# Turning the first group's queries inside the loop over the second group's products

## The chip, the cores and the metric

The kernel runs on one core of a Trainium2 chip. The metric is the device time of one execution in microseconds (us); lower is better. Three runs of the kernel before gave a median of 1921.63 us.

## The reference

The reference is a two-layer decoder trunk over 512 tokens and 16 meta tokens, width 1024. Layer 0 mixes tokens by gated linear attention; layer 1, which the change concerns, by sliding-window attention. Each layer is a SwiGLU block, the mixer and another SwiGLU block, each between two RMS norms, and everything is added to a residual. The mixer of layer 1, cut to what matters:

```python
def swa_mixer(hn, w_q, sinks, w_out, k, v, cos, sin):
    q = (hn @ w_q).reshape(B, L, N_KV_HEADS, GROUP, HEAD_DIM)
    q = apply_partial_rope(q, cos, sin) * HEAD_DIM ** -0.5      # first 16 of 64 columns are turned
    s = einsum(q_blk, k_band)        # own 128 keys, the 128 before, 16 meta keys
    p = sink_softmax(s, mask, sinks) # row maximum, exp, sum with a sink per head
    o = einsum(p, v_band)
    return o @ w_out
```

There are 16 query heads of 64 columns. Keys and values are made earlier and are shared.

## The kernel before

All activations lie transposed in on-chip memory: partitions are features, columns are tokens. A weight arrives by DMA in a `raw` buffer (eight of them), and ScalarE and VectorE make two rounded halves of it (L230 and L231, one pair of instructions for each half unit of 128x512); a product is then three matmuls (`mm3s`, L338).

The order of instructions on TensorE is written by hand, and a small planner (`Flow`, L64) decides what comes next. Jobs are Python generators. Each yields an estimated delay or another job to wait for, and `flow.clock` advances by an estimated cost per matmul. When a job's due time has come, its next step is recorded at that place, between two of the matmuls that the main thread is recording. So constants such as `GATHER`, `TURN` and `PROBS` (L50 to L52) are not waits on the chip: they move instructions to earlier or later places of every queue, TensorE's, VectorE's (DVE), ScalarE's (ACT), GpSimd's (POOL) and SyncE's (SP) alike. On the chip each engine works through its queue in order and waits on semaphores where data is not there yet.

The mixer of layer 1 is `swa` (L1121). Its steps:

1. `x_first` (L534) makes the queries of the first four of eight units (a unit is 128 features, that is two heads), for token group 0 (256 tokens) and then for group 1. After each group it spawns `drain`, which copies the four results from PSUM to `q` tiles on ACT (`evac`, L1145).
2. `turn` (L1148) applies the rotary turn to one half of the units and one group. It waits for the drain, then `GATHER`; four small matmuls with `sel` gather the 16 turned rows of each head in one PSUM tile, four DVE instructions turn them (L1159 to L1163), and eight DMAs on the SP queue put the rows back in the `q` tiles (L1167). It ends `TURN` later. Its first DVE instruction stands behind the last `x_l1m` operand that DVE builds (`after`, L1160).
3. `x_units` (L1289) makes the queries of the other four units, 512 tokens at a time: 32 steps of three matmuls. `turn(1, ...)` follows.
4. `attend(i)` is spawned for 16 visits. A visit is one unit and one half of the tokens; visits 0 to 3 are units 0 to 3 on the first half, 4 to 7 the same units on the second half, 8 to 15 the other units in the same way. `soft(i)` records the scores (16 matmuls into `sa` and `sb` tiles), two ACT copies (L1202), two DVE merges (L1203), the sink column and row maximum (L1215 to L1217), four exponentials on ACT (L1219) and the normalisation on DVE (L1224 to L1228). `core(i)` records, `NORM` after that, five transposes (L178, tiles `ptm` and `pt`), two ACT copies out of PSUM (L1240, L1248), one masked DVE copy (L1250), then, `PROBS` later, the products with the values (tile `o`) and the split of the result into `so` (L422 on ACT, L423 on DVE).
5. `out_proj` runs over units 0 to 3 when cores 0 to 7 have been recorded, and over units 4 to 7 at the end, where `Residual.run` puts in the row sums `st_post` and the factors `r_post`. Remaining visits are fed in between its matmuls.

Visit i's part on TensorE is called S(i) (its scores), T(i) (its transposes) and O(i) (its products with the values) below. They are recorded wherever the planner's clock says, and TensorE takes them in that order.

Of the kernel before, what the change touches and what calls it, by code (L numbers as in the profile page):

```python
# [29 lines left out]
L1 = [(16, 256), (272, 256)]  # L30
# [16 lines left out]
NORM = 5.0  # L47
LAG = 5
PERIOD = 4.5
GATHER = 3.0  # L50
TURN = 9.0
PROBS = 2.5  # L52
NEG = -1e30

V_GAIN = 0
# [72 lines left out]
def trunk_kernel(ctx: ExitStack, tc, a, out):  # L128
    nc = tc.nc
    pe, act, dve, pool, sp = nc.tensor, nc.scalar, nc.vector, nc.gpsimd, nc.sync  # L130
    flow = Flow()
# [16 lines left out]
    def ps(name):  # L148
        return pp.tile([P, 512], F32, tag="ps", name=name)
# [4 lines left out]
    def duo(name):  # L154
        t = pair_tile(name, F32)
        return t[:, 0], t[:, 1]
# [4 lines left out]
    def gain(layer, i, k):  # L161
        c = V_GAIN + layer * 48 + i * 8 + k
        return vec[:, c : c + 1]

    def mm(o, lhs, rhs, start=True, stop=True, onto=False, cost=None):
        inst = pe.matmul(o, lhs, rhs, start=start, stop=stop, skip_group_check=onto)  # L166
        n = 1
        for d in rhs.shape[1:]:
            n *= d
        flow.clock += cost or (n / 2400 if rhs.dtype == F32R else max(n / 600, 0.12))  # L170
        return inst

    def after(first, then):
        info = mybir.DependencyInfo(mybir.DependencyClass.NoSync, mybir.DependencyReason.DATA)
        tc.add_manual_dep(then.ins, first.ins.name, info, reason="order")
# [37 lines left out]
    def set_ahead(n, slots=None):  # L213
        ahead[0], limit[0] = n, slots or n
        room[0].finish(flow)
        room[0] = Job(None)
# [87 lines left out]
    def prefetch():  # L304
        while len(loaded) < cap[0] and asked[0] + costs[len(loaded)] <= freed[0] + ahead[0]:
            if isinstance(units[len(loaded)], list) and chains[0] == CHAINS:
                break
            load_unit()

    def next_w():  # L310
        used[0] += 1
        prefetch()
        flow.until(lambda: len(loaded) >= used[0])
        flow.wait(split_jobs[used[0] - 1])
        return loaded[used[0] - 1]
# [16 lines left out]
    def done_w(n=1):  # L332
        free_slots(sum(costs[released[0] : released[0] + n]))
        released[0] += n
# [3 lines left out]
    def mm3s(outs, j, x, g, start, stop, shared=False):  # L338
        t, n = g
        cols = slice(j % 4 * P, (j % 4 + 1) * P)  # L340
        xh, xl = x[:, 0, t : t + n], x[:, 1, t : t + n]
        for i, (o, w) in enumerate(outs):
            second = shared and i % 2 == 1
            mm(o, w[j // 4][:, 0, cols], xh, start and not second, False, second)
            mm(o, w[j // 4][:, 1, cols], xh, False, False, second)
        for i, (o, w) in enumerate(outs):
            second = shared and i % 2 == 1
            mm(o, w[j // 4][:, 0, cols], xl, False, stop, second)
            flow.pump()
# [181 lines left out]
        return late  # L531


    def x_first(x, nu, evac, opening=False, behind=(), first_ahead=8, held=None):  # L534
        behind = list(behind)
        ws = [] if opening else [next_w() for _ in range(nu)]
        set_ahead(8 if opening else 2 * first_ahead, held)
        jobs = []

        def drain(gi, g, some, pst):  # L540
            if x.column is None:
                yield x.rjob[gi]
            for i, p in zip(some, pst):
                evac(i, g, p)
                yield 0.6

        both = range(nu)
        order = [(0, both[: nu // 2]), (0, both[nu // 2 :])] if opening else [(0, both)]
        for gi, some in order + [(1, both)]:
            g = x.groups[gi]  # L550
            n = g[1]
            while len(ws) <= some[-1]:
                ws.append(next_w())
            shared = n <= 256
            if shared:
                banks = [ps(f"x{used[0]}_{i}_{gi}") for i in some[::2]]
                pst = [banks[i // 2][:, i % 2 * 256 : i % 2 * 256 + n] for i in range(len(some))]
            else:
                pst = [ps(f"x{used[0]}_{i}_{gi}")[:, :n] for i in some]
            for k in range(KD):  # L560
                x.need(gi, k)
                mm3s([(p, ws[i]) for i, p in zip(some, pst)], k, x.tiles[k], g, k == 0, k == KD - 1, shared)
            if x.column is None:
                flow.until(lambda: x.rjob[gi] is not None)
            jobs.append(flow.spawn(drain(gi, g, some, pst)))
            if gi == 0 and some[-1] == nu - 1:
                if held is None:
                    cap[0] = len(units)
                prefetch()
            if behind:  # L570
                flow.spawn(behind.pop(0))
        done_w(nu)
        return jobs
# [267 lines left out]
    def gla(x, finish):  # L841
        set_ahead(10)
        with tc.tile_pool(name="gp", bufs=1) as gp:
# [193 lines left out]

            kinds = [("lr", 0), ("k", 0), ("q", 0), ("v", 0)]
            drained = x_first(x, 4, lambda i, g, p: evac(*kinds[i], g, p), first_ahead=5)
            flow.spawn(resets())  # L1040
            gate = flow.spawn(gates(drained))
# [23 lines left out]
    def shared_kv(x, kp, behind):  # L1065
# [22 lines left out]
        def place(drained):  # L1088
# [26 lines left out]
            dve.tensor_tensor(dv, vt[:, 1:], vt[:, :3], op=ALU.subtract)  # L1115

        job = flow.spawn(place(x_first(x, 4, evac, behind=behind, first_ahead=6)))
        return (kz, vt, dv, vmz), job


    def swa(x, kv, finish):  # L1121
        kz, vt, dv, vmz = kv
        cap[0] = used[0] + 8
        with tc.tile_pool(name="ap", bufs=1) as ap:
# [23 lines left out]
            def turn(half, g, after_jobs):  # L1148
                for jb in after_jobs:
                    yield jb  # L1150
                yield GATHER
                o, n = g
                pk, sh = (t[:, o : o + n] for t in duo(f"turn{half}_{o}"))
                p = ps(f"turn{half}_{o}")[:, :n]
                for u in range(4):
                    mm(p[32 * u : 32 * u + 32], sel, qd[2 * half + u // 2][:, u % 2, o : o + n], cost=0.2)
                while (1, KD - 1) not in x.ready:
                    yield SCORE
                first = dve.stream_shuffle(sh, p, TURN_SHUFFLE)  # L1159
                after(x.built, first)  # L1160
                dve.tensor_tensor(pk, p, cr[:, o : o + n], op=ALU.mult)
                dve.tensor_tensor(sh, sh, sr[:, o : o + n], op=ALU.mult)
                dve.tensor_tensor(pk, pk, sh, op=ALU.add)  # L1163
                for u in range(4):
                    for e in range(2):
                        rows = qd[2 * half + u // 2][64 * e : 64 * e + 16, u % 2, o : o + n]
                        sp.dma_start(rows, pk[32 * u + 16 * e : 32 * u + 16 * e + 16])  # L1167
                yield TURN

# [61 lines left out]
            def core(i):  # L1231
# [18 lines left out]
                dve.tensor_tensor(own(ptc), own(pb), mle.unsqueeze(1).to_broadcast([P, 4 if hf else 2, P]), op=ALU.mult)  # L1250
                yield PROBS
                o = ps(f"o{u}_{hf}")
# [28 lines left out]
                paces.append(flow.spawn(pace(wait)))  # L1281
                cores.append(flow.spawn(core(i)))

            drained = x_first(x, 4, evac, held=12)
            set_ahead(16, 8)
            turns = [flow.spawn(turn(0, g, [drained[gi]])) for gi, g in enumerate(L1)]
            for i in range(8):
                attend(i, turns[i // 4], *cores[max(i - LAG, 0) : max(i - LAG + 1, 0)])
            x_units(x, 4, L1W, lambda i, g, p: evac(4 + i, g, p))  # L1289
# [16 lines left out]
    x = Operand("l0f0", lambda k: gain(0, 0, k), L0)  # L1306
# [54 lines left out]
    x = nxt  # L1361
    nxt, fin = into("l0f1", 0, 3, False, lambda k: gain(0, 4, k), L0)
    gla(x, fin)
    x = nxt
# [4 lines left out]
    with tc.tile_pool(name="kp", bufs=1) as kp:  # L1369
        x = Operand("l1f0", lambda k: gain(1, 0, k), L1)  # L1370

        def again(gi):
            for k in range(KD):
                x.build(gi, k)
                yield 1.0

        kv, placed = shared_kv(nxt, kp, [again(0), again(1)])
        x.rt, x.rjob = nxt.rt, nxt.rjob
        nxt, fin = into("l1m", 1, 1, True, lambda k: gain(1, 2, k), L1)
        roots = kp.tile([P, 2, 4], F32, name="roots")  # L1380
        nxt.column = [(roots[:, 0, 2 * g : 2 * g + 2], roots[:, 1, 2 * g : 2 * g + 2]) for g in range(2)]
        ffn(x, L1W, fin)
        x = nxt
        nxt, fin = into("l1f1", 1, 3, False, lambda k: gain(1, 4, k), L1)
        flow.wait(placed)
        swa(x, kv, fin)
# [91 lines left out]
```

## Time and profile before

| what | value |
|---|---|
| median of three runs | 1921.63 us (1921.38 to 1921.96) |
| profiled execution, its own time | 1919.54 us |
| span of its trace | 1917.7 us |
| granted TensorE clock, mean over the span | 0.994 |
| TensorE matmul busy | 1889.3 us, 99% |
| VectorE (DVE) busy | 1397.6 us, 73% |
| ScalarE (ACT) busy | 1016.4 us, 53% |
| GpSimd (POOL) busy | 178.9 us, 9% |
| DMA | 175.13 MB, mean 91 GB/s |

The profile is of one execution. Its own time is 2.1 us below the median of the runs, and the span is 1.8 us shorter than its time. "Idle before" is the time in which an engine had nothing to do ahead of an instruction, with what released it. The granted clock is the share of full speed at which TensorE was clocked. In the trace, a matmul of float32 operands appears as several records, so counts there are above those in the code; a busy TensorE is not TensorE at its peak.

The mixer of layer 1 stands between about 1388 us (its first query products) and 1550 us (the first products of the block behind it).

### The profile page before, as it was taken

The numbers are of one execution on the slowest core, as the hardware profiler recorded it, in microseconds if no ns is written. First come the engines' busy times: TensorE is split into PE (matmuls) and PEld (weight loads), VectorE is DVE, ScalarE is ACT, GpSimd is POOL, SyncE is SP. The second block draws the span as 40 slices with busy tenths as digits, with TensorE's granted clock in tenths as the row PEclk, the third lists the DMA queues.
The fourth block names the chain that finished last, engine by engine and source line by source line (L and its number), as shares of the span: only waits on it lengthen the run. The fifth ranks groups of instructions, "written<-read, shape, count | busy, mean of one in ns | idle before, by whom it ended". The sixth has DMA issues, their size and how long they took to land.

```text
span 1917.7 us, 37635 instructions
## 1 busy us (share of the span) xinstructions
PE 1889.3 (99%) x14658; PEld 1800.2 (94%) x14658; DVE 1397.6 (73%) x2803; ACT 1016.4 (53%) x2262; POOL 178.9 (9%) x379
## 2 busy tenths in 40 slices
PE   8999999999999999999999999999998999999997
PEld 8999999999999999999999898989986798989897
DVE  7885858665565788585878786868757678868584
ACT  5663636653246566363664553636647765636363
POOL 2000000321121300000031000000310040000002
PEclk9999999999999999999999999999998999999998
DMA  4332333322113123232341223333311212333331
GB/s 166 98 102 91 104 95 108 113 77 68 56 56 100 56 89 103 92 105 91 115 150 45 72 92 107 102 102 115 129 29 51 89 41 76 96 105 108 102 114 45
DMA packets 102932, 175.13 MB, mean 91 GB/s; under 512 B 11873, under 2 KB 24929, under 8 KB 102753
## 3 DMA queue, kind: packets, MB, share of 16 engines
q1 hardware_dynamic: 101920, 172.07, 28.5%
q8 instruction: 115, 1.88, 0.4%
q10 hardware_dynamic: 832, 0.65, 0.1%
q14 instruction: 65, 0.52, 0.1%
HBM read 170.05 MB, written 2.10 MB: 90 GB/s over the span
## 4 chain that ended last, share of the span: by engine, by line
PE 86%; DVE 9%; ACT 3%; issue 2%; DMA 1%; POOL 0%; SPq 0%; DVEq 0%; ACTq 0%
PE y L166 30%; PE x L166 18%; PE a L166 18%; PE c L166 8%; PE d L166 4%; DVE raw L255 2%; ACT w_s L249 1%; DVE w_s L250 1%; DVE w L250 1%; PE o L166 1%; PE e L166 1%; DVE w L231 1%; PE po L166 1%; PE ps L166 0%; DVE hidl1f L834 0%
## 5 line engine op out<-in xcount | busy, mean ns | idle before, releaser
L250 DVE TENSOR_TENSOR w_s<-raw,w_s 128x512 fp32r<-128x512 f32 x288 | 193.9, 690 | 130.0 <-ACT w_s L249 128.3
L166 PE MATMUL y<-hidl0f,w 128*128 128x256 f32 (+1 forms) x2112 | 261.9, 285 | 0.9 <-DVE hidl0f L423 0.6
L166 PEld LDWEIGHTS y<-hidl0f,w 128*128 128x128 f32 x2112 | 259.1, 188 | 1.6 <-DVE hidl0f L423 1.0
L249 ACT ACTIVATE w_s<-raw 128x512 fp32r<-128x512 f32 x288 | 175.3, 628 | 150.5 <-DVE raw L255 137.3
L231 DVE TENSOR_TENSOR w<-raw,w 128x512 fp32r<-128x512 f32 x378 | 236.3, 655 | 21.0 <-ACT w L230 19.0
L166 PE MATMUL y<-hidl1f,w 128*128 128x512 f32 (+1 forms) x1344 | 251.0, 346 | 0.3 <-DVE hidl1f L834 0.2
L166 PEld LDWEIGHTS y<-hidl1f,w 128*128 128x128 f32 x1344 | 212.3, 188 | 35.2 <-DVE hidl1f L834 1.5
L230 ACT ACTIVATE w<-raw 128x512 fp32r<-128x512 f32 x378 | 207.4, 586 | 41.1 <-PE y L166 30.4
L255 DVE TENSOR_TENSOR raw<-raw,raw 128x512 f32<-128x512 f32 x288 | 197.9, 687 | 5.6
L418 POOL TENSOR_TENSOR acc_post<-acc_post,sq_post 128x256 f32<-128x256 f32 (+1 forms) x72 | 58.9, 818 | 1469.4 <-ACT sq_post L417 1468.6
L250 DVE TENSOR_TENSOR w<-raw,w 128x512 fp32r<-128x512 f32 x216 | 148.2, 687 | 29.9 <-ACT w L249 29.2
L166 PE MATMUL x<-x_l0m,w 128*128 128x272 f32 (+1 forms) x1200 | 158.2, 288 | 0.0
L249 ACT ACTIVATE w<-raw 128x512 fp32r<-128x512 f32 x216 | 134.0, 621 | 41.3 <-PE y L166 41.0
L166 PEld LDWEIGHTS x<-x_l0m,w 128*128 128x128 f32 x1200 | 149.3, 189 | 1.1
L613 DVE TENSOR_TENSOR Y<-y,Y 128x256 f32<-128x256 f32 (+2 forms) x176 | 82.2, 473 | 71.9 <-PE y L166 71.5
L166 PE MATMUL a<-zl0f_t,w_s 128*128 128x264 f32 x864 | 117.5, 285 | 0.0
L166 PE MATMUL a<-zl1f_t,w_s 128*128 128x256 f32 x864 | 114.4, 281 | 0.9 <-ACT c L809 0.6
L166 PEld LDWEIGHTS a<-zl0f_t,w_s 128*128 128x128 f32 x864 | 110.3, 188 | 0.2
L166 PEld LDWEIGHTS a<-zl1f_t,w_s 128*128 128x128 f32 x864 | 107.2, 188 | 2.8 <-ACT c L809 2.4
L166 PE MATMUL x<-x_l0f,w 128*128 128x256 f32 (+1 forms) x768 | 100.5, 291 | 6.5 <-ACT w L230 5.9
L166 PEld LDWEIGHTS x<-x_l0f,w 128*128 128x128 f32 x768 | 97.1, 193 | 7.8 <-ACT w L230 5.9
L166 PE MATMUL x<-x_l1f,w 128*128 128x256 f32 (+1 forms) x576 | 92.6, 320 | 0.0
(484 smaller groups left out, 3250.8 us busy)
## 6 DMA issues: line engine op xcount, KB each, us to landing
raw<-in_w_in SPq DMA_DIRECT2D x352, 256.0 KB, 2.9
raw<-in_w_out SPq DMA_DIRECT2D x96, 256.0 KB, 3.3
raw<-in_gla_in SPq DMA_DIRECT2D x50, 256.0 KB, 3.1
raw<-in_w_last SPq DMA_DIRECT2D x48, 256.0 KB, 3.1
raw<-in_w_out SPq DMA_DIRECT2D x64, 128.0 KB, 2.9
raw<-in_gla_out SPq DMA_DIRECT2D x16, 256.0 KB, 2.8
raw<-in_w_q SPq DMA_DIRECT2D x16, 256.0 KB, 3.7
raw<-in_swa_out SPq DMA_DIRECT2D x16, 256.0 KB, 3.3
```

The lines of the kernel that those rows point to most:

```text
L166: inst = pe.matmul(o, lhs, rhs, start=start, stop=stop, skip_group_check=onto)
L230: act.activation(w[:, 0, :m], raw[:, :m], AF.Copy)
L231: dve.tensor_tensor(w[:, 1, :m], raw[:, :m], w[:, 0, :m].bitcast(F32), op=ALU.subtract)
L249: act.activation(w[:, 0, :512], src, AF.Copy)
L250: dve.tensor_tensor(w[:, 1, :512], src, w[:, 0, :512].bitcast(F32), op=ALU.subtract)
L255: dve.tensor_tensor(dst, dst, src, op=ALU.add)
L418: pool.tensor_tensor(sums[0][:, :n], sums[0][:, :n], t[:, :n], op=ALU.add)
L613: dve.tensor_tensor(y, p[:, :n], y, op=ALU.add)
```

## The change

`x_first` gets a callback, `then`, that it calls right after it has spawned a group's drain. `swa` uses it to spawn `turn` for that group at once. For group 0 this is ahead of the loop over group 1's products, for group 1 behind it. Before, both turns were spawned after `x_first` had returned. Three planner constants are changed too.

```diff
-GATHER = 3.0
-TURN = 9.0
-PROBS = 2.5
+GATHER = 2.0
+TURN = 8.5
+PROBS = 3.2
...
-    def x_first(x, nu, evac, opening=False, behind=(), first_ahead=8, held=None):
+    def x_first(x, nu, evac, opening=False, behind=(), first_ahead=8, held=None, then=lambda gi, job: None):
...
             jobs.append(flow.spawn(drain(gi, g, some, pst)))
+            then(gi, jobs[-1])
...
-            drained = x_first(x, 4, evac, held=12)
+            turns = []
+            x_first(x, 4, evac, held=12, then=lambda gi, job: turns.append(flow.spawn(turn(0, L1[gi], [job]))))
             set_ahead(16, 8)
-            turns = [flow.spawn(turn(0, g, [drained[gi]])) for gi, g in enumerate(L1)]
             for i in range(8):
                 attend(i, turns[i // 4], *cores[max(i - LAG, 0) : max(i - LAG + 1, 0)])
```

No instruction is added or removed. What changes is where the instructions of the turns, of the visits, and of some weight splits and loads stand in the queues of the engines. Behind L565 the lines of the changed kernel are numbered one higher, and behind L1286 again as before.

## The prediction

> **What bounds the kernel now.** I read the page's slices first (TensorE busy in nine tenths or more of nearly every slice), then three stretches of the mixer of layer 1: the query products with two scores among them, the visits with no large product beside them, and the visits among the output products.
>
> ```profile
> core 0: us, PE busy (x) PEld busy (x) DVE busy (x) ACT busy (x) POOL busy (x), PEclk, DMA share, GB/s
> 1404.20:1431.70 27.50, 27.50 (x156) 20.80 (x154) 7.86 (x23) 9.22 (x26) 2.34 (x12) 1.00 0.04 10
> 1431.70:1475.80 44.10, 37.74 (x369) 25.82 (x368) 36.05 (x96) 34.63 (x117) 0.00 (x0) 0.88 0.17 55
> 1475.80:1549.60 73.80, 73.24 (x596) 59.53 (x595) 45.31 (x117) 51.82 (x145) 8.78 (x12) 1.00 0.18 58
> ```
>
> Only in the middle stretch is TensorE idle (6.4 us) and slowly clocked (0.88), with DVE and ACT busy for 36.05 and 34.63 of 44.1 us. Its timeline shows the gaps:
>
> ```profile
> 1437.64 0.44 PE L166 MATMUL o<-pt,dv 128*64 128x128 f32 x4 [0.69 <-DVE pt L1250]
> ...
> 1443.41 0.69 PE L166 MATMUL o<-pt,vt 128*64 128x128 f32 x4 [1.37 <-ACT pt L1248]
> ...
> 1463.81 0.44 PE L166 MATMUL o<-pt,vt 128*64 128x128 f32 x4 [1.55 <-ACT pt L1248]
> ```
>
> O waits for the copies of what T put in PSUM. After such gaps the clock falls (the same columns, 2 us each):
>
> ```profile
> 1440.00:1442.00 2.00, 1.69 (x14) 1.35 (x14) 2.00 (x6) 2.00 (x6) 0.00 (x0) 1.00 0.89 257
> 1442.00:1444.00 2.00, 0.63 (x5) 0.30 (x4) 2.00 (x5) 1.94 (x6) 0.00 (x0) 0.65 0.93 318
> 1444.00:1446.00 2.00, 1.94 (x14) 0.88 (x12) 2.00 (x7) 1.02 (x5) 0.00 (x0) 0.50 0.93 327
> 1446.00:1448.00 2.00, 2.00 (x13) 1.31 (x11) 1.86 (x6) 1.51 (x8) 0.00 (x0) 0.50 0.68 215
> 1448.00:1450.00 2.00, 2.00 (x20) 1.80 (x20) 0.60 (x4) 0.95 (x3) 0.00 (x0) 0.65 0.23 51
> ```
>
> The lost shares (0.35+0.5+0.5+0.35) make 6.8 us at half clock from 1442.6; rows at 1466 and 1468 (0.62, 0.53) make 3.4 us more from 1466.5. In the 3.4 us ahead of each, 1.3 and 1.4 us are idle. At half clock an O took 3.25 us instead of 1.69, an S 1.87 instead of 1.14, a T 1.20 instead of 0.67.
>
> **The change, part by part.** The amount of work is the same; the sum is over what becomes idle or slow. The new places are those in which the built programs hold their instructions.
>
> *The first turn.* Its four matmuls move from among unit 4's products to group 1's products, some 18 matmuls of 0.12 us before their end, so to about 1402. TensorE executes them either way (0.57 us): nothing. Their data is old (copies end 1394.8). DVE is idle from 1402 to 1410, which hides the four turns (1.5 us), with one weight split now among them; two units' splits now stand behind the operand builds, finished by about 1406, and their weights are needed from 1419. Should that cover fail, TensorE waits at most for those, some 2 us. On SP five of eight `swa_out` loads pass ahead of the eight turn DMAs, three behind them; these loads are split only after 1435. The first DMA starts near 1404.8 and lands 1.8 us (median) later; S(0) is not reached before 1412.7, so 6 us of cover.
>
> *The visits.* S(0) moves from 1419.96 to about 1412.7 (first group's end 1404.8, sums 0.8, 27 matmuls of 0.241, a turn 0.57). Now S(0) to S(3), all of visit 0 and T(1) lie among query products, against S(0) and S(1) before. With T 0.67, S 1.14, O 1.69 (first half) or 1.91, the products end near 1436.3.
>
> *The order of a visit.* Before, TensorE took T(i), S(i+3), O(i): 1.14 us of scores beside the copies of T. Now, without a product near, it takes T(i), O(i), S(i+3). O(i) waits for ACT's copy (0.6) and for the masked copy on DVE, which starts only after that copy (1457.96 after 1456.73). What decides are the queues of DVE and ACT, worked out with these rows:
>
> ```profile
> 1458.56 0.15 DVE L1217 TENSOR_TENSOR nm<-nm,roots 128x4 f32<-128x4 f32 x1
> 1458.63 0.77 DVE L1203 COPY_PREDICATED s<-mgt,sb 128x256 f32<-128x256 int32 x2
> 1459.43 0.17 DVE L1215 TENSOR_TENSOR s<-vec,roots 128x4 f32<-128x4 f32 x1
> 1459.63 0.76 DVE L1216 TENSOR_REDUCE nm<-s 128x4 f32<-128x580 f32 x1
> 1460.42 0.16 DVE L1217 TENSOR_TENSOR nm<-nm,roots 128x4 f32<-128x4 f32 x1
> 1460.91 0.18 DVE L1224 RECIPROCAL den<-den 128x4 f32<-128x4 f32 x1 [0.33 <-ACT Y L1219]
> ```
>
> DVE: turn and splits first. From 1438.2 it has turn(1) 1.8+0.6, eight splits at 0.61, two merges at 0.67, two O splits at 0.33, two masked copies at 0.33, a reduction 0.67, a normalisation 0.6 and small ones 0.5: 11.7 us without a gap, to 1450.2, when masked copy 3 is done. Before, it was done at 1453.6: the start is 3.4 us ahead. Then one visit's loop, in DVE's new order from one masked copy to the next: reduction 0.79; 0.25 to the exponentials; 2.10 to the reciprocal (1458.81 to 1460.91); it, the mean row and the O split 0.75; two merges 0.67; normalisation 0.6 and sinks 0.1; masked copy 0.6: 5.8 us. DVE waits out the exponentials in each loop, since nothing stands between maximum and reciprocal; before, the previous visit's masked copy or the next one's merges often did, and the four loops to masked copy 7 took 5.1 us each (1453.6 to 1474.1). Now 1450.2 + 4 x 5.8 = 1473.4. O(7) follows the masked copy with 1.55 us, so the output products start at 1475.05, not 1475.83; but S(10), 1.14 us, was done by then and is not now. Net +0.4 us: the lead is spent in the loops. The bounds: loops of 5.1 as measured give -2.4; a wait for ACT of 0.3 us in each gives +1.6.
>
> *The end.* T(15) now stands behind all but six of the first group's matmuls (0.73 us), and the row sums `st_post` directly after these and ahead of O(15). They need the last `Y`, which DVE adds only behind masked copy 15. From T's end: ACT's queue and copy 0.9, masked copy 0.6, add 0.34, ACT's square 0.2+0.4 and latencies 0.3, so 2.7 us; TensorE arrives after 0.73: +1.9 us. Before, O(15) and 21 matmuls hid this chain; no gap is shown there. Bounds 1.2 (if the copy is early) to 3.
>
> *The clock.* Each loop of 5.8 us holds about 2.0 us of idle TensorE (1.2 before O, 0.8 between its halves), and 1441.6 to 1449.7 holds 4.7. The first certainly crosses the 1.3 to 1.4 us in 3.4 that was enough before; the loops do in about half of the phases. A slow O(3) delays the exponentials queued behind its split on ACT: +1.5 (3.25 less 1.69). A slow loop has scores 1.6 and O 2.6 on its path and grows by 1.25, four loops half of the time +2.5; the wait at `st_post` may cost 1 more. That is 5.0 at most likely phases, nothing if the clock holds. I take 3.0: the gaps are spread more evenly than the old ones, one of which (1.24 us in 3.4) did not slow the clock.
>
> Sum: +0.4 +1.9 +3.0 = +5.3 us on an own time of 1919.54 (span 1917.7 and 1.8 around it), so 1924.8; the median of runs lies 2.1 above this execution, so **1927.0**.
>
> **Rivals.** *The clock stays full*: if only one gap of a whole 3.4 us counted, no new gap (longest 2 us, before T(3)) would slow it: +0.4+1.9 = +2.3, 1923.9. Against it: the longest old gap is 1.55 us and the clock fell twice. [...]
>
> *Faster*: ACT and DVE overlap as before and TensorE sets the pace. A loop is then 0.67+0.9+1.69 to 1.91+1.14, 4.6 us; four from 1450.2 end at 1468.6, 5.5 us ahead of before; less S(10), and with `st_post` fed early, -4.4: 1917.2. For it: the lead of 3.4 us is real. Against: DVE's order. It decides if masked copies come under 5 us apart.
>
> *A lost cover in front* (the turn late on SP or DVE, TensorE waiting in group 1's products): up to 2 us more, 1929. Against: 6 us of cover.
>
> *No effect*: the early turn only makes S(0) earlier and the gaps merely shift; the change does not do what it says: 1921.6. Against: four scores instead of two under the products.
>
> **How the numbers follow.** 0.2% is 3.8 us, about what a measurement can tell from no change. Forecast 0.52, clock stays full 0.25, faster 0.15, lost cover 0.05, no effect 0.03. Forecast and lost cover lie beyond +3.8 but for 0.02 of them: slower 0.55; same 0.30 with the clock's rival and no effect; faster 0.15. The forecast's own range is 1925 to 1931 (clock terms 1 to 7); 1918.5 to 1931.5 takes in the clock's rival, the front's cost and the better part of the faster case.
>
> **What would show it.** S(0) near 1412.7; O(3) to O(7) with a gap ahead of each from ACT's or DVE's `pt`; masked copies 5.8 us apart or more; granted clock at half for three or more windows of 3.4 us after 1441; a gap of about 2 us at `st_post`. Masked copies 5 us apart, or a full clock, would make it wrong.

## The result, and the profile after

The changed kernel takes 1934.58 us (median of six runs, 1933.42 to 1936.33), the kernel before 1921.6 us on the same chip: 13.0 us more, a ratio of 1.0069 with a 95% interval of 1.0056 to 1.0081. The direction was forecast; the size was not (1927.0, range 1918.5 to 1931.5).

The profiled execution took 1936.33 us of its own time (span 1934.5), 16.8 more than that of before; its mean granted clock is 0.987 against 0.994. It is the longest of the six, and the one of before lies 2.1 us below its median, so the traces show somewhat more loss than the medians. The three stretches of the mixer, cut at the same marks as before (end of the first group's products, end of the query products, first output product, first product of the next block):

```profile
core 0: us, PE busy (x) PEld busy (x) DVE busy (x) ACT busy (x) POOL busy (x), PEclk, DMA share, GB/s
1404.96:1436.90 31.94, 31.94 (x209) 24.71 (x207) 14.30 (x40) 15.70 (x46) 2.78 (x12) 1.00 0.15 42
1436.90:1481.38 44.48, 35.56 (x291) 23.17 (x291) 29.20 (x76) 29.38 (x97) 0.00 (x0) 0.74 0.18 54
1481.38:1567.13 85.75, 82.14 (x612) 66.67 (x611) 49.48 (x126) 53.19 (x147) 10.21 (x14) 0.90 0.16 50
```

The first stretch has no gap; it ends 5.2 us later than before because more of the visits lies in it. The second should have become shorter by as much, and did not: TensorE idles for 8.9 us in it (6.4 before) at a clock of 0.74 (0.88). The third grew from 73.8 to 85.75 us, of which 1.14 is S(10), moved into it; it now has 3.6 us of idle and a clock of 0.90, where before had 0.56 and 1.00. The next block then starts 17.5 us late (1567.13 against 1549.65), of which 16.8 us are left at the end.

The gaps, from TensorE's timeline (start, duration, engine, line; in brackets the idle time and what ended it):

```profile
1449.71 0.69 PE L166 MATMUL o<-pt,vt 128*64 128x128 f32 x4 [0.69 <-ACT pt L1249]
...
1471.96 0.44 PE L166 MATMUL o<-pt,vt 128*64 128x128 f32 x4 [0.69 <-ACT pt L1249]
...
1477.21 0.44 PE L166 MATMUL o<-pt,vt 128*64 128x128 f32 x4 [0.97 <-ACT pt L1249]
1478.46 0.69 PE L166 MATMUL o<-pt,dv 128*64 128x128 f32 x4 [0.81 <-DVE pt L1251]
...
1532.43 0.44 PE L166 MATMUL o<-pt,vt 128*64 128x128 f32 x4 [1.99 <-ACT pt L1249]
1533.20 0.69 PE L166 MATMUL o<-pt,dv 128*64 128x128 f32 x4 [0.33 <-DVE pt L1251]
...
1549.66 1.00 PE L166 MATMUL st_post_l1f<-ones,acc_post 128*128 128x1 f32 x6 [1.28 <-ACT acc_post L414]
```

O(3), O(6) and O(7) wait as foretold (these are their rows; O(4) and O(5) do too), and so does `st_post`. The longest single wait, 1.99 us ahead of O(13), was in no part of the prediction. The granted clock in rows of 2 us, same columns as above:

```profile
1446.00:1448.00 2.00, 0.33 (x2) 0.20 (x3) 2.00 (x5) 2.00 (x9) 0.00 (x0) 0.94 0.80 267
1448.00:1450.00 2.00, 1.31 (x8) 0.91 (x8) 2.00 (x6) 1.32 (x4) 0.00 (x0) 0.50 0.85 260
1450.00:1452.00 2.00, 2.00 (x16) 1.01 (x12) 1.39 (x7) 0.00 (x0) 0.00 (x0) 0.50 0.74 249
...
1532.00:1534.00 2.00, 1.24 (x10) 0.67 (x12) 1.93 (x6) 2.00 (x6) 0.74 (x1) 0.78 0.90 307
1534.00:1536.00 2.00, 2.00 (x16) 1.13 (x16) 1.81 (x3) 1.14 (x3) 0.72 (x1) 0.50 0.65 237
```

Such rows give the spans at half clock: from 1447.8 (6.8 us), 1458.0 (13.7), 1478.5 (6.8), 1533.1 (6.8, behind O(13)'s wait) and 1550.2 (6.8, behind `st_post`'s). That is 41 us, against 10.2 before. The starts lie 10.2, 20.5, 54.6 and 17.1 us apart, which is 3, 6, 16 and 5 steps of 3.41 us: in this trace the clock falls on a fixed grid, so whether a gap counts may depend on where it lies on that grid.

What half clock does to a visit's loop is to be seen on DVE, from one masked copy (L1251) to the next:

```profile
1464.22 0.69 DVE L1251 TENSOR_TENSOR pt<-pt,mle 128x512 f32<-128x512 f32 x1 [0.34 <-ACT pt L1249]
1464.83 0.75 DVE L1217 TENSOR_REDUCE nm<-s 128x4 f32<-128x580 f32 x1
1465.61 0.16 DVE L1218 TENSOR_TENSOR nm<-nm,roots 128x4 f32<-128x4 f32 x1
1467.97 0.18 DVE L1225 RECIPROCAL den<-den 128x4 f32<-128x4 f32 x1 [2.20 <-ACT s L1220]
...
1470.17 0.79 DVE L1204 COPY_PREDICATED s<-mgt,sb 128x256 f32<-128x256 int32 x2 [1.32 <-PE sb L166]
...
1471.94 0.69 DVE L1251 TENSOR_TENSOR pt<-pt,mle 128x512 f32<-128x512 f32 x1 [0.34 <-ACT pt L1249]
```

DVE waits out the exponentials (2.20), as foretold, and then once more, 1.32 us, for the scores: behind O, at half clock, they come later than the exponentials end. The loop is 7.72 us long; those from masked copy 3 on were 6.9, 7.4, 7.7 and 5.8.

### The profile page after: what moved, and what is told of

Its sections match the earlier page's. It is cut to its first block, busy times and chain, and to the rows that moved or that the text cites. A ratio compares the mean times of both kernels' runs of the same rounds, so it can differ in the third digit from the quotient of the medians.

```text
span 1934.5 us, 37618 instructions
## 1 busy us (share of the span) xinstructions
PE 1900.3 (98%) x14658; PEld 1807.9 (93%) x14658; DVE 1397.4 (72%) x2803; ACT 1017.5 (53%) x2262; POOL 179.3 (9%) x379
## 4 chain that ended last, share of the span: by engine, by line
PE 85%; DVE 9%; ACT 3%; issue 1%; POOL 0%; DMA 0%; SPq 0%; DVEq 0%; ACTq 0%; POOLq 0%
PE y L166 29%; PE x L166 18%; PE a L166 18%; PE c L166 8%; PE d L166 4%; DVE raw L255 2%; PE o L166 2%; ACT w_s L249 1%; DVE w_s L250 1%; DVE w L250 1%; PE e L166 1%; DVE w L231 1%; PE po L166 1%; PE sa L166 1%; PE ps L166 0%
```

## The experiments

The theory after the result: the early turn itself costs nothing; early turn and new constants together turn TensorE's order from T, S, O to T, O, S where no large product hides it, and put waits at the end; the gaps then pull the clock down, and that costs more than the gaps. Each run below is compared with the kernel before on its own chip (1919.64 us for the first four, 1919.74 for the next four, 1919.99 for the last two).

**The early turn with the old constants.** Edit:

```diff
-GATHER = 2.0
-TURN = 8.5
-PROBS = 3.2
+GATHER = 3.0
+TURN = 9.0
+PROBS = 2.5
```

> The early turn with the three constants of before (GATHER 3.0, TURN 9.0, PROBS 2.5). In its program the stretch without products runs T(i), S(i+3), O(i) again, as before, and st_post stands three matmuls behind O(15), past the row-sum chain. Theory A (the order T, O, S and the late end, both made by the constants, cost the time; the early turn itself costs nothing): 1916 to 1923 us, at most 7 us of half clock between 1437 and 1480, no gap at O(13). Rival B (the early turn itself costs, by what it pushes in front of the visits): within 3 us of the changed kernel's 1934.6.

1917.48 us, ratio 0.9986 (0.9977 to 0.9995). This kernel beats both: the early turn alone is a small gain of 2.2 us (1 to 4 by the interval). TensorE's order is T, S, O again, and the output products start at 1474.16, 1.7 us ahead of before.

**The new constants without the early turn.** Edit: the three constants of the change in the kernel before.

> The three new constants (GATHER 2.0, TURN 8.5, PROBS 3.2) with the turn spawned where it was before. In its program the stretch without products still runs T, S, O. Theory A (order): 1919 to 1925 us, as the old kernel, since the constants alone do not turn the order round. Rival B (early turn costs): the same 1919 to 1925. Rival C (the constants cost wherever the turn stands, for example PROBS 3.2 by the later T(14) and T(15)): 1927 or more.

1919.06 us, ratio 0.9995 (0.9986 to 1.0004): nothing that can be measured. Neither half of the change costs time; only both together do.

**Filling the gaps, first trial.** Matmuls of a tile of zeros, 0.128 us each (0.06 had been expected), into columns of the `ptm` and `o` banks that hold no result yet. Edit:

```diff
+            def fill(bank, n, first=True):
+                for k in range(n):
+                    mm(bank[:, 256:384], zeros, zeros, first, False, onto=True, cost=1e-9)
...
+                if i == 3:
+                    fill(pm, 18)
...
+                if 2 <= i < 8:
+                    fill(o, 12)
...
+                    if 4 <= i < 8 and c == 0:
+                        fill(o, 10, False)
```

> The changed kernel with small matmuls of zeros into unused columns of PSUM tiles: 12 ahead of O(2) to O(7), 10 between the halves of O(4) to O(7), 18 ahead of T(3), about 0.06 us each, so 0.6 to 1.1 us into gaps of 0.7 to 1.2 us. Nothing else is moved. If the half clock is a price of its own beside the idle time: the granted clock stays at 1.00 from 1437 to 1480, the output products start near 1476 instead of 1481.4, and the time falls by 4 to 7 us, to 1928 to 1931. If the waits for DVE and ACT are all there is: no gain, or up to 2 us slower by the added matmuls.

1934.04 us, ratio 1.0073 (1.0057 to 1.0088): no gain, though the clock's mean rose to 0.994. The trace shows why this run decides nothing. The fills were longer than the gaps: from 1460 us on, at full clock, the loops are 6.41 us, without a gap, all TensorE. And they moved ACT's queue: the copy of T(3) came behind four exponentials,

```profile
1454.54 0.69 PE L166 MATMUL o<-pt,vt 128*64 128x128 f32 x4 [4.69 <-ACT pt L1255]
```

and O(3) waited 4.69 us for it. It is repeated below with short fills.

**The row sums later.** Edit: one planner delay of the residual behind the mixer is longer, so `st_post` of the first group is recorded behind O(15). The delay holds for the second group too, whose row sums also move back.

```diff
-            yield 1.8
+            yield 3.0 if self.name == "l1f1" else 1.8
```

> The changed kernel with one planner delay raised from 1.8 to 3.0 for the residual behind the mixer, which moves st_post from ahead of O(15) to three matmuls of the second token group behind it; the rest of TensorE's order is the same. If st_post's wait costs what the trace shows there (1.3 us idle and 6.8 us at half clock behind it): 3 to 4.5 us less than the changed kernel, 1930 to 1931.5. If only the idle counts: 1 to 1.5 us less. If the wait is hidden by what follows: no change within 0.7 us.

1934.78 us, ratio 1.0070 (1.0053 to 1.0087): no change. The wait at `st_post` and the half clock behind it are gone, and the next block starts at 1561.98 instead of 1567.13 us. But 23 us into that block its products wait for their operand, which a chain from the row sums builds (waits of 0.39 and 0.30 us stand shortly ahead of this one):

```profile
1589.25 4.61 PE L166 MATMUL x<-x_l1f,w 128*128 128x256 f32 x18 [1.66 <-ACT x_l1f L442]
```

and the clock falls for 3.4 us there. The wait was moved, not removed. In the trace 48 TensorE records of the next block stand ahead of the second group's row sums, 33 in the changed kernel, so this edit may itself have made the later wait; the run doesn't tell what the wait at `st_post` alone costs.

**The new order in the stretch, the old end.** Edit: `PROBS` back to 2.5, the other two constants as changed. 24 output products stand between T(13) and O(13) instead of 33, twelve between T(15) and O(15), the row sums behind O(15); up to O(7) TensorE's order is that of the changed kernel.

> The changed kernel with PROBS back at 2.5, GATHER 2.0 and TURN 8.5 kept. TensorE still takes T(i), O(i), S(i+3) in the stretch with no large product beside it (that half of the new order is kept), while from T(13) on its order is that of the early turn with the old constants: 24 output products between T(13) and O(13), 12 between T(15) and O(15), the row sums behind O(15). Theory 'both halves pay': the output products start about 5.5 us late as in the changed kernel (near 1481), but the 2.0 us before O(13), the 1.3 us before the row sums and the two half-clock spans of 6.8 us behind them are gone (about 3.3 of idle, 1.1 to 1.9 us lost to each slow span): 1927 to 1929. Rival 'the end is all': the late start of the output products is made up later, 1919 to 1922. Rival 'the stretch is all': the end's waits were hidden by work that was late anyway, 1933 to 1935.

1926.73 us, ratio 1.0032 (1.0019 to 1.0044), just below the 1927 to 1929 of 'both halves pay'. Against its kernel before that is +7.0 where the changed kernel has +13.0: 6.0 us of the loss were at the end. Its stages (same columns; the cuts are the first output product and the next block):

```profile
1436.90:1479.89 42.99, 33.76 (x297) 21.91 (x294) 29.57 (x79) 29.33 (x97) 0.00 (x0) 0.81 0.18 56
1479.89:1557.52 77.63, 76.80 (x612) 61.76 (x611) 48.58 (x124) 52.79 (x146) 9.74 (x13) 0.97 0.17 56
```

In O(13) there is one wait of 0.72 us, none at `st_post`, no half clock behind 1484; the first row is nearly as slow as in the changed kernel (1.5 us shorter).

**The old order in the stretch, `PROBS` new.** Edit: `GATHER` and `TURN` back to 3.0 and 9.0, `PROBS` 3.2 kept.

> The changed kernel with GATHER and TURN back at 3.0 and 9.0, PROBS kept at 3.2. TensorE takes T(i), S(i+3), O(i) in the stretch, as before the change; the end is between the two: 27 products between T(13) and O(13), 24 between T(15) and O(15), the row sums 6 products behind O(15). Theory 'the order T, O, S in the stretch starts the loss': the output products start as with the early turn and the old constants (near 1474 to 1475) and hardly any time is lost behind them: 1917 to 1920. Rival 'PROBS at 3.2 makes the loss by what it does to the end': 1923 to 1929. Rival 'nothing but the early turn counts': 1917.5 exactly as with the old constants.

1918.37 us, ratio 0.9990 (0.9981 to 0.9999). TensorE's order is T, S, O, there is no gap behind 1470, and the loss is gone. The output products start at 1476.46, later than expected, behind two spans of 6.8 us at half clock, and that costs nothing that can be measured. So with the early turn `GATHER` and `TURN` decide the order in the stretch; `PROBS` at 3.2 does harm only together with them, and then behind the stretch.

**Short fills.** The changed kernel with the fills of the first trial cut to the gaps' size; ACT's and DVE's queues keep their order but for a few neighbours. Edit, against the first trial:

```diff
+FILL_O = {2: 6, 3: 5, 4: 6, 5: 6, 6: 6, 7: 6, 13: 12}
+FILL_M = {4: 4, 5: 4, 6: 4, 7: 4}
...
-                if i == 3:
-                    fill(pm, 18)
...
-                if 2 <= i < 8:
-                    fill(o, 12)
+                fill(o, FILL_O.get(i, 0))
...
-                    if 4 <= i < 8 and c == 0:
-                        fill(o, 10, False)
+                    if c == 0:
+                        fill(o, FILL_M.get(i, 0), False)
```

> The changed kernel with short runs of matmuls of a tile of zeros into unused columns of the o bank (0.128 us each): five or six ahead of O(2) to O(7), four between the halves of O(4) to O(7), twelve ahead of O(13). They add 6.5 us of TensorE work, all of it in places where TensorE stood idle in the changed kernel; ACT's and DVE's queues keep their order but for a few neighbours behind visit 7 (the first trial with fills was longer than the gaps and moved the exponentials ahead of the copies of T(3)). Theory 'the half clock has a price of its own': without gaps the clock stays full, the loops come down from 6.9 to 7.7 us to about 6, the output products start near 1476 and the spans of half clock behind them are gone: 1923 to 1927. Rival 'the queues of DVE and ACT set the loops, whatever the clock': loops of about 7 us stay, 1933 to 1936.

1926.27 us, ratio 1.0032 (1.0021 to 1.0043). The fills are 63 matmuls or 8 us more of work on TensorE, and the loss against the kernel before is 6.5 us instead of 13.0. The profiled execution took 1932.67 us, 6.4 above the median, with 27 us at half clock, so its rows don't stand for the median; still, two of its loops, from masked copy 4 to 6, ran at full clock and are 5.77 and 5.76 us.

**Fills in the kernel with the early turn and the old constants.** Edit: nine such matmuls ahead of O(2) and O(6) there.

> The early turn with the old constants (1917.5 us), with nine such matmuls of zeros (1.15 us) ahead of O(2) and ahead of O(6), where TensorE stood idle for 1.38 and 1.55 us; ACT's and DVE's queues are unchanged. That kernel has one span of 6.8 us at half clock, from about 1444 on. Theory 'the half clock has a price of its own': the span goes, 1915 to 1916.5. Rival 'DVE and ACT set the pace there': 1917 to 1918.5, the same within what can be measured.

1918.63 us, ratio 0.9992 (0.9983 to 1.0001), 1.15 us above the same kernel without fills: a miss. One gap was filled and the other cut to 0.40 us, but the clock fell none the less, from 1445.8 for 6.8 us and from 1469.7 for 3.4. So this run tells nothing of the price of half clock, and it shows that filling the longest gaps does not always hold the clock.

**The new order, the old end, short fills.** Edit: the kernel of 1926.73 us, with `FILL_O` and `FILL_M` as above but for O(13), and `fill(pm, 6)` ahead of T(3). ACT's queue is unchanged.

> The kernel with the order T, O, S in the stretch and the old end (1926.7 us), with short runs of matmuls of zeros in the stretch alone: six ahead of T(3), five or six ahead of O(2) to O(7), four between the halves of O(4) to O(7); ACT's queue is unchanged. It asks what the order costs without the half clock, and what the half clock adds to it. Theory 'the order costs a little, the half clock doubles it': loops of 5.8 us from masked copy 4 on, output products from about 1476.5, 1921 to 1924. Rival 'the order alone makes the 7 us': 1926 to 1928. Rival 'all of it is the half clock': 1918 to 1920.

1921.63 us, ratio 1.0008 (0.9998 to 1.0017). This run separates best: the new order with no half clock from 1436 to 1600 in its profiled execution (1920.29 us).

```profile
1436.90:1475.23 38.33, 33.65 (x351) 24.35 (x350) 29.00 (x77) 27.43 (x92) 0.00 (x0) 1.00 0.21 63
1475.23:1551.07 75.84, 75.00 (x613) 60.41 (x612) 48.46 (x124) 54.05 (x150) 9.38 (x13) 1.00 0.18 57
```

One of its loops on DVE, from masked copy (L1259 here) to masked copy:

```profile
1461.12 0.68 DVE L1259 TENSOR_TENSOR pt<-pt,mle 128x512 f32<-128x512 f32 x1
1461.72 0.74 DVE L1219 TENSOR_REDUCE nm<-s 128x4 f32<-128x580 f32 x1
1462.50 0.16 DVE L1220 TENSOR_TENSOR nm<-nm,roots 128x4 f32<-128x4 f32 x1
1464.86 0.18 DVE L1227 RECIPROCAL den<-den 128x4 f32<-128x4 f32 x1 [2.20 <-ACT s L1222]
...
1465.55 0.77 DVE L1206 COPY_PREDICATED s<-mgt,sb 128x256 f32<-128x256 int32 x2
...
1466.88 0.68 DVE L1259 TENSOR_TENSOR pt<-pt,mle 128x512 f32<-128x512 f32 x1
```

The wait for the exponentials is the same 2.20 us; the one for the scores (1.32 us at half clock) is gone. 5.76 us against 7.72 for the same loop: half clock adds 1.96. The profiled executions of this kernel and of the one without fills (spans of 1918.5 and 1924.9 us) differ by 6.4 us, and by 20.5 us at half clock: an estimate from the two is 0.3 us lost for each microsecond at half clock.

**The changed kernel, more fills.** Edit: the short fills, `fill(pm, 6)` ahead of T(3) and fourteen instead of twelve ahead of O(13).

> The changed kernel with the short runs of zeros as in the trial of 1926.3 us, and six more ahead of T(3), fourteen instead of twelve ahead of O(13). What is left is the order T, O, S at (nearly) full clock and the two waits at the end (2.3 us ahead of O(13), filled but not shortened, and 1.3 us ahead of the row sums). Theory 'half clock and waits add up': 1923 to 1926, the output products from 1476 to 1477. Rival 'the queues set the time': 1926 to 1928, no change against the trial before.

1925.27 us, ratio 1.0036 (1.0020 to 1.0052). Against the run above it has the new end, and is 3.6 us slower. The waits at the end explain 2.9 us of that: 1.99 and 0.33 in O(13) and 1.28 at `st_post` in the changed kernel, less the 0.72 in O(13) that the run above has as well. That they do is argued from these sizes; the trace is of an execution of 1932.27 us, with 27 us at half clock, and not of one near the median. The granted clock goes with a large difference here: six executions took 1923.0 to 1926.0 us at a mean clock of 0.995 to 0.996, three took 1932.3 to 1933.7 at 0.991. The same program with the same queues takes 8 us more where its mean clock is 0.004 to 0.005 lower.

## Why the prediction was right in direction and wrong in size

Differences of medians, each to the kernel before on its own chip, give these steps from the kernel before to the changed one. By their intervals each median is good to about 2 us (that of 1925.27 to 3), so a step is good to 3 or 4, and the last two are not clear of noise. The recorded ratios give -2.7, +4.2, +4.6, +5.4 and +1.8 for the same steps.

| step | from | us |
|---|---|---|
| early turn alone | 1917.48 | -2.2 |
| order T, O, S, clock full | 1921.63 against that | +3.8 |
| half clock in the stretch | 1926.73 against 1921.63 | +5.4 |
| end: mostly waits at O(13) and `st_post` | 1925.27 against 1921.63 | +3.6 |
| the rest, taken to be half clock at the end | what is left of 13.0 | +2.4 |

*The front: right.* S(0) came at 1412.77 (1412.7 forecast); no gap in the first stretch, so nothing was late on DVE or SP; that rival is out.

*The order of a visit: right.* Masked copy 3 was done at 1450.3 (1450.2 forecast; the terms listed there add up to 1449.9 and, for the output products, to 1474.95, so a few tenths of the agreement are luck). The loops of 5.8 us are those of the full clock: 5.76 where fills keep it. There the output products start at 1475.23, forecast 1475.05, with S(10) still to come. The net of +0.4 is +1.6 in time (the early turn's -2.2 and the order's +3.8; the kernel with the early turn alone has 6.8 us at half clock and the filled one none, so the order's own price may be somewhat higher). "Faster" is refuted on its own condition, masked copies under 5 us apart.

*The end: half seen.* The wait at `st_post` is 1.28 us (1.9 forecast, 1.2 to 3 as bounds). The walk stopped at T(15) and missed T(13) to O(13), where the reason is on ACT's queue:

```profile
1525.50 3.75 ACT L230 ACTIVATE w<-raw 128x512 fp32r<-128x512 f32 x7
1529.14 0.50 ACT L1220 ACTIVATE s<-s,nm,roots 128x145 f32<-128x145 f32 x1
...
1531.11 0.62 ACT L230 ACTIVATE w<-raw 128x512 fp32r<-128x512 f32 x1
1531.63 0.27 ACT L1241 ACTIVATE pm<-ptm 64x128 f32<-64x128 f32 x1
1531.79 0.59 ACT L1249 ACTIVATE pt<-pt 128x512 f32<-128x512 f32 x1
```

T(13) was done at 1526.5. Its copy `pt` stands behind eight weight splits (4.4 us) and the exponentials of visit 15. With `PROBS` at 2.5 the splits stand behind the copy, and the gap of 1.99 us is not there:

```profile
1527.30 0.58 ACT L1249 ACTIVATE pt<-pt 128x512 f32<-128x512 f32 x1
1527.77 4.26 ACT L230 ACTIVATE w<-raw 128x512 fp32r<-128x512 f32 x8
```

The waits in O(13) are 2.3 us, against 0.72 in that kernel: the term that was missing is 1.6 us.

*The clock: the step that failed.* Its signs came true: gaps ahead of O(3) to O(7), and twelve windows of 3.4 us at half clock where at least three were named. But it was sized at 3.0, with 7 as the upper end, and is about 7.7 us (5.4 and 2.4; 6.4 by the ratios). This is the largest part of the miss; the wait in O(13) and the order's price make up the rest. The traces agree: by the estimate of 0.3 us for each microsecond at half clock, the 31 us more of it in the profiled execution cost some 9 us of its 16.8. The number lay low for three reasons that the runs show. First, "half of the phases" for the loops: in the profiled execution, the longest of the six, three of four were slow. Second, the growth of a slow loop was put at 1.25 and is 1.1 to 2.0, since the scores stand behind O on TensorE and at half clock come later than the exponentials. Third, the waits at the end bring half clock of their own (13.6 us there), for which the prediction had 1 us. The reason given for the low number, that the gaps are spread more evenly than the old ones, did not hold.

The rival "the clock stays full" summed up to +2.3 us. The clock did not stay full; with most of it restored, the changed kernel takes 5.3 us more than its kernel before, and 1.6 us of the difference are O(13)'s, which were not in that sum. Its condition, that only a gap of a whole 3.4 us counts, no run shows: the spans at half clock are 3.4, 6.8 and 13.7 us long, but `st_post`'s gap of 1.28 us is all the idle time in the 3.4 us ahead of the fall at 1550.2.

Why the planner turns the order around only with both edits together stays open beyond what the runs with `GATHER`, `TURN` and `PROBS` show.

## What to carry to other kernels

Where TensorE idles in short gaps inside a small-matmul stretch like this one, price the gaps twice: once as idle time, once as half clock on what follows (here an estimated 0.3 us for each microsecond at half clock), and test the second by filling the gaps with matmuls that nobody reads. When a constant of a planner moves work, walk the queue of every engine to each late consumer, not only at the place that the change is about: eight weight splits ahead of one copy made 1.6 us of wait here, most of what the early turn alone brings (2.2). Two edits that cost nothing alone can make an order together that neither makes, so try them apart before they are kept together.

## What the runs showed of the hardware

The granted clock fell with far less than 3.4 us of idle time in the 3.4 us ahead of it. They held 1.3 and 1.4 us of idle time in the kernel before, 1.3 to 2.2 in the changed kernel, and 0.56 to 0.76 at some falls in the kernels with fills. (Ends of matmuls are modelled, so these are rough.) But idle time alone does not decide: with the new constants alone 1.6 us of idle, from 1460.1 to 1463.5, did not bring the clock down. What else decides stays open. Between 1430 and 1600 us half clock came in spans of 3.4 us and its multiples, mostly 6.8, and within a trace falls and rises stand whole steps of 3.41 us apart there: seven steps between the two falls in the kernel before, 3, 6, 16 and 5 in the changed kernel.

Work added to TensorE made a kernel faster: 8 us of matmuls of zeros halved the loss of the changed kernel, from 13.0 to 6.5 us.
